# A running log-sum-exp over the rows of four matrices: loads and stores put into the DMA queue two at a time

## The chip, the cores and the metric

The kernel runs on one core of a Trainium2 chip. The metric is the device time of one execution in microseconds (us), lower is better. A core has five engines that run beside one another, each in its own program order: TensorE (PE, matrix multiply; its weight loads are listed as PEld), VectorE (DVE), ScalarE (ACT, functions of one argument), GpSimd (POOL) and SyncE (SP). In this kernel SP does nothing but issue DMAs. Sixteen DMA engines carry the data between the DRAM and the core's memory.

## The reference

The input `x` has the shape (4, 4096, 4128) in 32-bit floats: four batches of 4096 rows. Each output row is the logarithm of the sum of the exponentials of all rows up to it in its batch.

```python
def reference(x):
    B, S, D = x.shape
    out = np.zeros_like(x)
    out[:, 0, :] = x[:, 0, :].copy()
    for t in range(1, S):
        mx = np.maximum(out[:, t - 1, :], x[:, t, :])
        out[:, t, :] = mx + np.log(np.exp(out[:, t - 1, :] - mx) + np.exp(x[:, t, :] - mx))
    return out.astype(np.float32)
```

Every element is read once and written once, 270.53 MB each way.

## The kernel before

**Steps.** The rows of a batch are cut into steps. A step is 384 rows (128 partitions with r = 3 consecutive rows in each) or 256 rows (r = 2). A batch has ten steps of 384 rows and one of 256; the small one comes first in batch 0 and last in the others. There are 44 steps in all, numbered here from 0; the small ones are 0, 21, 32 and 43. A step of 384 rows moves 6192 KB in and as much out, a small one 4128 KB.

**Buffers.** A step lives in one tile `xt` of the pool `xpool`, which has `bufs = 4` buffers. `Step.load` (L132) fills it, the compute works in place, and `Step.store` (L135) writes it out. So load k+4 goes into the buffer of step k, and can't be issued before store k has landed. Both are issued on SP, one after another in the order in which the program emits them. A wait on SP holds up everything behind it on SP.

**Chunks.** The 4128 columns of a step are four chunks of 1024; the last chunk takes the remaining 32 columns (the tail) along. For each chunk:
- `exp` (L147, ACT) computes the exponentials in half precision over the front half of the same columns of the tile.
- `later` (L155, VectorE) adds the exponentials of the second and third row of each partition into the tile `sum`, when r is 3.
- `head` (L163 to L177, TensorE) builds in a PSUM tile `pt` the sum of all rows before the partition, the partition's first row, and the carry of the step before. `tail_head` does the same for the tail.
- `stage(j)` (L198) takes the logarithm of `pt` on ACT into row j of `xt`, then has TensorE add row j+1 (L201). After the last row it calls `keep` (L111, L112), which saves the running sum in `carry` for the next step, on VectorE. L203 is the logarithm of the tail.

**Order.** The schedule is written out by hand (`manual_schedule`): each engine runs its instructions in the order of emission, and the framework adds the waits on semaphores that the data needs. The main loop (L229) runs over all chunks g. In each iteration it emits `later` for chunk g+1, then `stage(2)` of chunk g-2, `stage(1)` of g-1 and `stage(0)` of g, then `exp` of chunk g+2 and `head` of g+1. So the last `stage` of a step stands on ACT behind the exps of the first chunks of the next step, and these need the next load.

**DMA order.** Four loads are issued ahead of the loop (L222, L223). When the last stage of step k has been emitted, the program emits store k and behind it load k+3, for k from 1 on (L236 to L240). SP's order is therefore: load 0, 1, 2, 3, store 0, store 1, load 4, store 2, load 5, and so on to store 40, load 43, store 41, store 42, store 43.

Of the kernel before, what the change touches and what calls it, by code (L numbers as in the profile page):

```python
# [50 lines left out]
def kernel(  # L51
# [23 lines left out]
    bufs = 4  # L75
# [132 lines left out]
    steps = []  # L208
# [9 lines left out]
        assert row == S  # L218

    chunks = [Chunk(s, c) for s in steps for c in range(n_main)]  # L220
    ahead = bufs - 1
    for s in steps[:bufs]:  # L222
        s.load()  # L223
    stored = 0
    chunks[0].exp()
    chunks[1].exp()
    chunks[0].later()
# [1 line left out]
    for g in range(len(chunks) + R - 1):  # L229
        if g + 1 < len(chunks):  # L230
            chunks[g + 1].later()
        for d in range(R - 1, -1, -1):
            if 0 <= g - d < len(chunks) and d < chunks[g - d].t.r:
                k = chunks[g - d]
                k.stage(d)
                if k.c == last and d + 1 == k.t.r:  # L236
                    k.t.store()
                    if bufs <= stored + ahead < len(steps):
                        steps[stored + ahead].load()
                    stored += 1  # L240
        if g + 2 < len(chunks):
            chunks[g + 2].exp()
        if g + 1 < len(chunks):
            chunks[g + 1].head()
# [30 lines left out]
```

## Time and profile before

| | |
|---|---|
| time, median of 3 runs | 1262.99 us (1262.85 to 1263.17) |
| the profiled execution: its own time | 1263.19 us |
| its span, first to last instruction | 1261.5 us |
| ACT busy | 947.3 us |
| PE busy | 661.2 us |
| DVE busy | 647.7 us |
| moved by DMA | 541.44 MB, mean 429 GB/s over the span |

The span is what the profile covers; the 1.7 us between it and the execution's own time lie around it. A group line of the profile gives: source line, engine, operation, output<-input, shapes, number of instructions, then busy time, mean duration in ns of one, and the idle time of the engine just before them with what ended most of it. A line of the timeline gives: start in us from the start of the span, length in us, engine, source line, operation, operands. For a DMA the length is that of its issue on SP (written SPq), not of the transfer; the DMA view gives the time from issue to landing, that is until the last of the 16 engines has reported:

| issued at L132 or L135 | number | KB each | median us from issue to landing |
|---|---|---|---|
| loads | 40 | 6192.0 | 42.3 |
| stores | 40 | 6192.0 | 28.1 |
| small loads | 4 | 4128.0 | 37.4 |
| small stores | 4 | 4128.0 | 29.7 |

A line of the waits gives: who waited, for whom, the total in us, how many times, and the longest.

### The profile page before, as it was taken

Reading aid. Unit: us, or ns where it says so; the run is one execution under the profiler, and the core shown is the slowest. Engines: PE = TensorE matmul, PEld = TensorE weight load, DVE = VectorE, ACT = ScalarE, POOL = GpSimd, SP = SyncE. Lnnn points to the kernel's source line nnn. Section 1 sums busy time; section 2 is a strip of 40 time slices with the busy share of each in tenths; the row PEclk is TensorE's granted clock in tenths of the full one; section 3 lists DMA queues with packets and bytes.
Section 4 is the critical chain, followed back from the end, with each engine's and each line's share of the span. In section 5 each row is a group of like instructions: output and inputs, shape, how many; then the busy total and the mean of one; then the engine's idle time right before and its main releaser. Section 6 shows DMA issues by size and latency. Waiting matters only on the chain. (4 is left out here: it accounts for less than half of the span.)

```text
span 1261.5 us, 5926 instructions
## 1 busy us (share of the span) xinstructions
PE 661.2 (52%) x1948; PEld 236.7 (19%) x1948; DVE 647.7 (51%) x606; ACT 947.3 (75%) x733; POOL 2.2 (0%) x13
## 2 busy tenths in 40 slices
PE   3655545465555555555446554555534655544562
PEld 1222111122121111211112121111111221111120
DVE  2674445554555545545446545544544645544454
ACT  5997777777777777778669777777866977777784
POOL 0000000000000000000000000000000000000000
PEclk9987676766577776768757677766775767787666
DMA  9999999999999999999999999999999999999998
GB/s 410 410 437 434 429 430 437 431 430 431 440 430 431 430 439 430 431 433 431 438 433 435 428 432 438 432 430 431 434 435 430 435 427 436 434 434 429 437 416 346
DMA packets 12702, 541.44 MB, mean 429 GB/s; under 512 B 1408, under 2 KB 1408, under 8 KB 1408
## 3 DMA queue, kind: packets, MB, share of 16 engines
q1 hardware_dynamic: 12672, 541.07, 99.4%
q8 instruction: 15, 0.25, 0.1%
q14 instruction: 15, 0.12, 0.0%
HBM read 270.53 MB, written 270.53 MB: 429 GB/s over the span
## 5 line engine op out<-in xcount | busy, mean ns | idle before, releaser
L147 ACT ACTIVATE xt<-xt 128x3072 f16<-128x3072 f32 (+3 forms) x176 | 478.3, 2717 | 248.4 <-DMA xt<-in_x_dram 248.4
L198 ACT ACTIVATE xt<-pt 128x1024 f32<-128x1024 f32 x512 | 487.5, 1029 | 2.5 <-PE pt L101 0.7
L155 DVE TENSOR_TENSOR sum<-xt 128x1024 fp32r<-128x1024 f16 x160 | 196.0, 1225 | 531.2 <-ACT xt L147 406.7
L97 PE MATMUL pt<-xt,ident 128*128 128x512 f16 x176 | 82.9, 471 | 482.8 <-ACT xt L198 482.8
L111 DVE CAST carry<-pt 32x1024 f16<-32x1024 f32 x176 | 216.4, 1230 | 46.4 <-ACT xt L198 41.3
L101 PE MATMUL pt<-xt,ident 128*128 128x512 f16 x496 | 209.5, 495 | 28.4 <-ACT xt L198 28.1
L112 DVE TENSOR_TENSOR carry<-pt,carry 32x1024 f16<-32x1024 f32 x176 | 215.9, 1226 | 6.1
L167 PE MATMUL pt<-sum,excl_r 128*128 128x512 f32 x320 | 198.7, 716 | 0.0
L101 PEld LDWEIGHTS <-ident 128*128 128x128 f16 x496 | 52.4, 106 | 646.5 <-issue 636.1
L97 PE MATMUL pt<-xt,incl 128*128 128x512 f16 x176 | 95.7, 544 | 71.7 <-DVE carry L112 54.0
L167 PEld LDWEIGHTS pt<-sum,excl_r 128*128 128x128 f32 x320 | 95.4, 298 | 48.4 <-issue 31.1
L101 PE MATMUL pt<-xt,incl 128*128 128x512 f16 x176 | 99.2, 564 | 0.0
L97 PE MATMUL pt<-carry,pick 128*128 128x512 f16 x160 | 84.4, 528 | 0.0
L101 PE MATMUL pt<-carry,pick 128*128 128x512 f16 x160 | 79.4, 496 | 0.0
L97 PEld LDWEIGHTS <-incl 128*128 128x128 f16 x220 | 23.7, 108 | 192.7 <-DVE carry L112 167.0
L203 ACT ACTIVATE xt<-qt 128x96 f32<-128x96 f32 (+1 forms) x44 | 10.9, 249 | 46.3 <-PE pt L101 46.3
L97 PEld LDWEIGHTS <-pick 128*128 128x128 f16 x200 | 24.2, 121 | 67.0 <-issue 66.3
L101 PEld LDWEIGHTS <-incl 128*128 128x128 f16 x260 | 27.6, 115 | 12.7 <-issue 9.2
L97 PEld LDWEIGHTS <-ident 128*128 128x128 f16 x176 | 21.4, 122 | 30.3 <-issue 24.3
L101 PEld LDWEIGHTS <-pick 128*128 128x128 f16 x160 | 20.5, 128 | 2.4 <-issue 1.7
L111 DVE CAST carry_t<-qt 32x32 f16<-32x32 f32 x44 | 8.7, 197 | 13.7 <-ACT xt L203 13.5
L97 PE MATMUL qt<-xt,incl 128*128 128x96 f16 (+1 forms) x44 | 10.6, 240 | 0.0
(25 smaller groups left out, 79.8 us busy)
## 6 DMA issues: line engine op xcount, KB each, us to landing
xt<-in_x_dram SPq DMA_DIRECT2D x40, 6192.0 KB, 42.3
out_dram<-xt SPq DMA_DIRECT2D x40, 6192.0 KB, 28.1
xt<-in_x_dram SPq DMA_DIRECT2D x4, 4128.0 KB, 37.4
out_dram<-xt SPq DMA_DIRECT2D x4, 4128.0 KB, 29.7
```

Source lines behind the costliest of these rows:

```text
L97: nc.tensor.matmul(pt, lhsT=w, rhs=rhs, start=start, stop=stop, skip_group_check=True)
L101: pe.add_instruction(mybir.InstMatmult(name=nc.get_next_instruction_name(), ins=[pe.lower_ap(rhs), pe.lower_ap(w, for_matmul_weights=True) ...
L111: nc.vector.tensor_copy(cr[HI:HI + 32, :], pt[HI:HI + 32])
L112: nc.vector.tensor_tensor(out=cr[LO:LO + 32, :], in0=pt[HI:HI + 32], in1=cr[HI:HI + 32, :], op=mybir.AluOpType.subtract,)
L147: nc.scalar.activation(self.t.half[:, :, 2 * c0:2 * c0 + w], self.t.xt[:, :, c0:c0 + w], ACT.Exp,)
L155: nc.vector.tensor_tensor(out=self.sum, in0=self.e(1, 0, CH), in1=self.e(2, 0, CH), op=mybir.AluOpType.add,)
L167: nc.tensor.matmul(pt[:, s:s + MM], lhsT=excl_r, rhs=self.sum[:, s:s + MM], start=False, stop=False, skip_group_check=True,)
L198: nc.scalar.activation(t.xt[:, j, c * CH:(c + 1) * CH], pt, ACT.Ln)
L203: nc.scalar.activation(t.xt[:, :, t0:D], self.qt, ACT.Ln)
```

## The change

Stores and loads are no longer emitted step by step. With `group = bufs // 2`, which is 2, nothing is emitted after an even step; after the last stage of an odd step k the program emits store k-1, store k, load k+3 and load k+4. SP's order becomes: load 0, 1, 2, 3, store 0, 1, load 4, 5, store 2, 3, load 6, 7, and so on to store 38, 39, load 42, 43, store 40, 41, store 42, 43. The buffers, the compute and its order on the other engines, `later` on VectorE among it, stay as they are.

```diff
@@ -218,10 +218,10 @@
     chunks = [Chunk(s, c) for s in steps for c in range(n_main)]
-    ahead = bufs - 1
+    group = bufs // 2
     for s in steps[:bufs]:
         s.load()
-    stored = 0
+    stored = done = 0
     chunks[0].exp()
@@ -234,10 +234,13 @@
                 k = chunks[g - d]
                 k.stage(d)
                 if k.c == last and d + 1 == k.t.r:
-                    k.t.store()
-                    if bufs <= stored + ahead < len(steps):
-                        steps[stored + ahead].load()
-                    stored += 1
+                    done += 1
+                    if done % group == 0 or done == len(steps):
+                        for s in steps[stored:done]:
+                            s.store()
+                        for s in steps[stored + bufs:done + bufs]:
+                            s.load()
+                        stored = done
```

## Prediction

> **What bounds the kernel now.** I read the page's summary first, then the chain of waits, then the DMA issues, and last the SP queue's waits and the timeline of its issues. Steps are numbered 0 to 43; steps 0, 21, 32 and 43 move 4128 KB each way, the others 6192 KB.
>
> ```profile
> span 1261.5 us, 5926 instructions
> PE 661.2 (52%) x1948; PEld 236.7 (19%) x1948; DVE 647.7 (51%) x606; ACT 947.3 (75%) x733; POOL 2.2 (0%) x13
> DMA  9999999999999999999999999999999999999998
> q1 hardware_dynamic: 12672, 541.07, 99.4%
> DMA 16%; ACT 5%; issue 1%; PE 1%; DVE 0%; SPq 0%; ACTq 0%
> L147 ACT ACTIVATE xt<-xt 128x3072 f16<-128x3072 f32 (+3 forms) x176 | 478.3, 2717 | 248.4 <-DMA xt<-in_x_dram 248.4
> ```
>
> The queue that SP feeds keeps the 16 DMA engines busy for 99.4% of the span. ACT, the busiest compute engine, is idle a quarter of it, and 248.4 us of that idleness is an exp waiting for a load. So the transfers bound the time, and an edit matters only if it lets the queue run dry, or changes how long a transfer takes.
>
> Is the queue really served back to back? The timeline of SP in mid-run (start, length, line):
>
> ```profile
> 292.29 0.37 SPq L132 DMA_DIRECT2D xt<-in_x_dram  x1
> 321.13 0.33 SPq L135 DMA_DIRECT2D out_dram<-xt  x1
> 321.57 0.37 SPq L132 DMA_DIRECT2D xt<-in_x_dram  x1
> 350.38 0.33 SPq L135 DMA_DIRECT2D out_dram<-xt  x1
> ```
>
> The DMA view, cut to each of these, gives 42.2, 28.0, 42.1 and 28.0 us to landing. So load 12 lands at 334.5, store 10 at 349.1, load 13 at 363.7, store 11 at 378.4: one transfer every 14.6 or 14.7 us, in the order of issue. When store 10 is issued, load 12 still has 334.5 - 321.1 = 13.3 us to run: that is the cover.
>
> What sets the issue of a store? Load 11 landed at 263.02 + 42.2 = 305.2, and store 10 went out 15.9 us later. ACT's timeline shows why: it stops 6.0 us before the first exp of step 11, and the last Ln of step 10 stands behind that exp on ACT. One step is then 276.02 to 299.3, some 23.3 us of ACT. So step k is done either 15.9 us after load k+1 lands (ACT waiting), or 23.3 us after step k-1 (ACT not waiting).
>
> **The change, part by part.** The instructions are the same: 44 loads, 44 stores, the same waits by buffer, the same compute. Only SP's order changes, from S10 L13 S11 L14 to S10 S11 L14 L15. A load still takes the buffer of the store four steps back, but now that store stands just ahead of it, not four issues ahead.
>
> *Waits on SP.* I place the new order on time, with T the landing of load 4. Loads 4 and 5 go in a pair, so load 5 lands at T+14.6. Behind load 5 SP comes to store 2. Load 2 landed a period of four transfers, 58.5 us, before T; steps 2 and 3 are 46.6 us of ACT, so ACT stands waiting when load 4 lands. By the two rules above, step 1 is done at T-58.5+15.9 = T-42.6, step 2 at T-42.6+23.3 = T-19.3, step 3 at T+15.9. Load 5 waits for store 1, which lands at T-14.6; store 2 follows it at once, and lands at T+29.2. Store 3 waits for step 3 until T+15.9 and is needed at T+29.2: cover 13.3 us, the same as now. Load 6 waits for store 2 to land at T+29.2; store 3 is then in flight, so the cover is 14.6 us. Load 7 waits for store 3, with load 6 in flight: 14.6 again. Store 4, behind load 7, is long done. Queued behind each waiting load on SP are only the next load and the next stores; who waits for them is ACT's next exp, which has 58.5 - 46.6 = 12 us per pair to spare. Cost 0.
>
> Without that cover a wait would cost the start of an empty queue: load 0, issued first, needs 12.3 us where a transfer of its size lands 9.7 us after the one ahead (the last store: 1245.28 + 15.3, against 1234.77 + 16.1), so 2.6 us each time.
>
> The trace has such a wait already:
>
> ```profile
> SPq L135 <- ACT xt L198: 1177.8, 44, 30.0
> SPq L132 <- DMA out_dram<-xt: 17.4, 5, 5.1
> ```
>
> Five loads do wait for a store to land. One is load 23, issued at 608.13, just as store 19 lands (584.53 + 23.5 = 608.0). Store 20 ahead of it lands at 606.45 + 31.0 = 637.5, load 23 at 608.13 + 43.9 = 652.0: 14.6 later. Nothing was lost. What the transfer ahead hides stays hidden.
>
> [...]
>
> *Issues.* 88 of 0.33 to 0.42 us in either order, under at least 13 us of queued work. Cost 0.
>
> *Runs of one direction.* The queue turns between reading and writing half as often. Loads alone: load 1 lands at 1.23 + 26.5 = 27.7, load 2 at 1.70 + 40.6 = 42.3, 14.6 apart. Store behind store: store 0 at 37.25 + 31.8 = 69.1, store 1 at 63.69 + 20.0 = 83.7, 14.6. Mixed, from store 2 (113.8) to store 40 (1183.01 + 28.4 = 1211.4) 38 pairs took 1097.6 us with four small transfers, each 4.9 shorter: (1097.6 + 19.6) / 38 = 29.4, against 2 x 14.6 = 29.2. If all of this 0.15 to 0.2 is turning, the gain has a bound of 0.15 x 39 = 6 us. On the other side, load 3, the last of the opening run, lands at 58.3, 16.0 after load 2: 1.4 us over. Should every read run end so, 20 x 1.4 = +28 us. The nearest rows are the many single handovers in mid-run at 14.6 to 14.7 either way, so I take -0.5.
>
> *Front and end.* The first two stores and load 4 are as now (load 4 waits for store 0 either way). At the end load 43 comes right behind load 42, so ACT's last wait goes:
>
> ```profile
> 1221.49 1.91 ACT L147 ACTIVATE xt<-xt 128x2048 f16<-128x2048 f32 x1 [1.64 <-DMA xt<-in_x_dram]
> ```
>
> Store 42 can then be issued up to 1.6 us before 1234.77. But store 41 lands at 1212.43 + 23.6 = 1236.0 and store 42 at 1250.9, 14.9 later where 14.6 is the floor: worth 0 to 0.3, I take 0.1.
>
> **Sum.** 0 + 0 - 0.5 - 0.1 = -0.6 us. The profiled execution took 1263.19 us (span 1261.5 and 1.7 around it), 0.2 over the median of 1262.99, so the forecast is 1262.99 - 0.6, rounded to 1262.5; its own range, from a third of the turning gain to a little new loss, is 1260.5 to 1265.
>
> **Rivals.** *The pair is one wait*: the first store of a pair leaves only when the second step is done. Then store 2 goes out at T+15.9, after load 5 has landed at T+14.6, into an empty queue: 15.9 + 2.6 - 14.6 = 3.9 us in each of 19 groups, 74 us; store 0 would go at 63.7 and land at 63.7 + 2.6 + 9.7 = 76.0, 7 late; store 42 would go at 1245.3 and the end come 1245.3 + 2.6 + 14.6 - 1250.9 = 11.6 late. In all +93, 1356 us. For it: the code emits both stores behind the last Ln of the second step. Against it: a store now waits for its own buffer, not for what was emitted before it. Step 10's last stage emits carry copies ahead of the store, and VectorE runs the first after it:
>
> ```profile
> 321.89 1.23 DVE L111 CAST carry<-pt 32x1024 f16<-32x1024 f32 x1
> ```
>
> The point of decision: it costs as soon as the first store leaves over 12.0 us (14.6 - 2.6) after the pair's first load lands.
>
> *A read run ends badly*, as load 3 did: +28, 1291 us. For it that one row; against it that load 3 ended at the first store of the kernel, and later handovers don't show it.
>
> *The engines drift apart*, and those ahead run dry while a load waits for the slowest engine's part of a store: from 1226 to 1236 the DMA share is 0.58, so by the end the mean engine stood 4.2 us idle waiting for store 42. The cover of 14.6 less 4.2 and 2.6 still leaves 8, and the slowest engine sets the end; a piece of it might cost 5 us, 1268.
>
> *Turning was the cost*: -6, 1257 us. For it the 0.2 us per pair; against it that the engines are 99.4% occupied as it is.
>
> **Chances.** Forecast 0.72, one wait for the pair 0.10, read runs 0.04, drift 0.05, turning 0.09. About 0.2%, 2.5 us, is what a measurement of this kernel can tell from no change. Under 1260.5 lie turning and a sliver of the forecast: 0.10. Over 1265.5 lie the first three rivals and a sliver: 0.20. Within: 0.70. The range from 1257.5 to 1268 takes in the forecast, half of turning and most of drift, and leaves some 0.18 outside.
>
> **What would show it.** SP's timeline: two stores, two loads; the first store of a pair right behind the second load, not 0.4 us ahead of its partner (else the first rival). Loads waiting for stores on SP for 13 to 15 us each, some 40 times, with landings still 14.6 apart (else turning, drift or read runs). The DMA share stays 1.00 and 433 GB/s in mid-run. ACT waits for loads once per pair, about twice as long each time, in the same total. The forecast is wrong if the DMA row drops below 9 in any slice before the last, or if the pair of transfers leaves 29.4 us.

## The result and the profile after

The changed kernel takes 1266.97 us (median of 7 runs, 1266.19 to 1268.04), against 1262.77 us for the kernel before (1262.68 to 1263.17): a ratio of 1.0032, with a 95% interval of 1.0021 to 1.0044. It is 4.2 us slower. The forecast was 1262.5 us, practically no change, so it was wrong: the time lies above the forecast's own range (1260.5 to 1265), though inside the wider one that it gave (1257.5 to 1268).

The page of the changed kernel, in the lines that answer to those shown of the kernel before. The profiled execution took 1268.04 us, the longest of the seven.

```profile
span 1266.3 us, 5926 instructions
PE 630.6 (50%) x1948; PEld 228.7 (18%) x1948; DVE 647.7 (51%) x606; ACT 945.3 (75%) x733; POOL 2.2 (0%) x13
DMA  9999999999999999999999999999999999999997
q1 hardware_dynamic: 12672, 541.07, 99.2%
DMA 70%; ACT 18%; issue 4%; PE 4%; DVE 2%; SPq 0%; ACTq 0%; DVEq 0%
L147 ACT ACTIVATE xt<-xt 128x3072 f16<-128x3072 f32 (+3 forms) x176 | 478.7, 2720 | 259.3 <-DMA xt<-in_x_dram 259.3
```

The compute has the same instructions, and the DMA row is as full as before up to the last slice. The page gives no hint of where 4.2 us went: the queue is busy nearly all the time, but the same bytes take longer. SP's timeline and its waits show the new order at work:

```profile
1053.88 15.22 SPq L132 DMA_DIRECT2D xt<-in_x_dram  x2
1069.20 30.36 SPq L135 DMA_DIRECT2D out_dram<-xt  x2
1112.93 15.19 SPq L132 DMA_DIRECT2D xt<-in_x_dram  x2
```

```profile
SPq L135 <- ACT xt L198: 660.2, 33, 29.9
SPq L132 <- DMA out_dram<-xt: 511.9, 38, 19.6
```

Two loads, two stores. The second load of a pair goes out at 1068.77, and the first store right behind it at 1069.20. Loads wait for a store to land 38 times, 13.5 us on average, and until the last stores the slowest engine always had work.

To find the time one must leave the page for the landings. A transfer lands when the last of its 16 DMA engines reports (the page counts 1408 packets under 512 bytes, 16 for each of the 88 transfers). The even-numbered loads have exactly the same transfers ahead of them in both kernels, so their landings can be compared. The table gives, from the records of the trace, when the 15th and the 16th engine reported (us):

```
              before             after         16th engine,
           15th      16th     15th      16th   after - before
load 8    216.36   216.96   215.11   215.88      -1.08
load 20   568.57   568.61   567.36   570.03      +1.42
load 30   852.71   853.13   851.48   855.24      +2.11
load 34   964.84   966.05   965.25   969.40      +3.35
load 38  1076.94  1078.87  1078.53  1083.30      +4.43
load 42  1194.56  1196.56  1196.34  1201.34      +4.78
store 43 1260.54  1260.62  1263.44  1265.47      +4.85
```

The changed kernel is 1.08 us ahead at load 8 and loses 5.9 us from there to the end. Until load 30 the 15th engine is no later than before; one engine falls behind alone, by 3.8 us at load 30. Between loads 30 and 38 all engines lose time. At the end the lag is passed on: store 42 waits for step 42, step 42 for load 42, so store 42 is issued at 1237.67 instead of 1234.77, and the other engines wait for work with it.

The packets of that one engine can be followed, each starting 3 ns before the one ahead ends. A packet of 49,536 bytes normally takes 1829 ns, eight make a transfer. Its load packets mostly do (the table of all traces below has 26 ns over per load before and 15 after). These are the ns over 1829 of the store packets, with the instructions that PE, PEld, DVE and ACT ran in that time (in two windows each; an instruction that crosses the bound between them counts in both, and counted once they are 52, 89 and 70):

```
                          packets 1 to 8               sum   instructions
before, store 39 (1166.7) 15  5  0 44 33 33 15 43      188   57
after,  store 36 (1097.4) 27 33 15 43 43 43 52 43      299   91
after,  store 37 (1112.4) 32 38  5 33 43 33 33 33      250   72
```

The instruction counts come from these windows (bounds, length, then busy time and count of PE, PEld, DVE, ACT, POOL; granted clock; DMA share; GB/s), first the kernel before, the first three packets of store 39 and the other five:

```profile
1166.70:1172.20 5.50, 0.40 (x2) 0.12 (x2) 2.21 (x2) 5.04 (x4) 0.00 (x0) 0.56 1.00 432
1172.20:1181.50 9.30, 7.21 (x17) 2.36 (x16) 5.55 (x7) 8.20 (x7) 0.00 (x0) 0.50 0.99 426
```

and the changed kernel, stores 36 and 37:

```profile
1097.40:1103.00 5.60, 3.32 (x12) 1.40 (x12) 3.68 (x3) 5.60 (x5) 0.00 (x0) 0.94 1.08 469
1103.00:1112.40 9.40, 4.69 (x23) 1.76 (x22) 6.69 (x6) 9.01 (x8) 0.00 (x0) 0.97 1.02 443
1112.40:1117.90 5.50, 3.18 (x8) 1.08 (x7) 2.86 (x5) 4.76 (x5) 0.00 (x0) 0.75 0.97 417
1117.90:1127.20 9.30, 6.83 (x18) 2.47 (x17) 5.57 (x5) 9.27 (x7) 0.00 (x0) 0.72 1.00 431
```

Before, 10 instructions run under the first three packets, and these are hardly lengthened; 47 run under the other five. In store 36 it is 32 and 59. The reason is where the compute pauses. In the kernel before it pauses once per step, as a load ends and a store begins: ACT has just begun again, and PE is still idle:

```profile
1171.81 0.59 PE L97 MATMUL pt<-xt,ident 128*128 128x512 f16 x1 [7.51 <-ACT xt L198]
```

In the changed kernel it pauses once per pair, twice as long, and the pause lies under loads (this load lands at 1083.3, the stores come 14.6 us later):

```profile
1083.38 2.76 ACT L147 ACTIVATE xt<-xt 128x3072 f16<-128x3072 f32 x1 [13.86 <-DMA xt<-in_x_dram]
```

So theory A, formed here: **each instruction that the compute engines run lengthens the store packets of one DMA engine by some 3 ns** (188 / 57, 299 / 91, 250 / 72 give 3.3, 3.3 and 3.5; with each instruction counted once, 3.4 to 3.6), the load packets of that engine hardly at all. The pairs put the busy time of the compute under the stores and its pause under the loads.

### The profile page after: what moved, and what is told of

Same layout as the page of the kernel before. It is cut to its first block, busy times and chain, and to the rows that moved or that the text cites. A ratio compares the mean times of both kernels' runs of the same rounds, so it can differ in the third digit from the quotient of the medians.

```text
span 1266.3 us, 5926 instructions
## 1 busy us (share of the span) xinstructions
PE 630.6 (50%) x1948; PEld 228.7 (18%) x1948; DVE 647.7 (51%) x606; ACT 945.3 (75%) x733; POOL 2.2 (0%) x13
## 2 busy tenths in 40 slices
DMA packets 12702, 541.44 MB, mean 428 GB/s; under 512 B 1408, under 2 KB 1408, under 8 KB 1408
## 3 DMA queue, kind: packets, MB, share of 16 engines
q1 hardware_dynamic: 12672, 541.07, 99.2%
## 4 chain that ended last, share of the span: by engine, by line
DMA 70%; ACT 18%; issue 4%; PE 4%; DVE 2%; SPq 0%; ACTq 0%; DVEq 0%
DMA out_dram<-xt 40%; DMA xt<-in_x_dram 30%; ACT xt L198 9%; ACT xt L147 8%; PE pt L101 2%; PE pt L97 1%; DVE carry L111 1%; DVE carry L112 1%; DVE sum L155 0%; PE pt L167 0%; ACT xt L203 0%; SPq L132 0%; ACTq L273 0%; ACTq L147 0%; ACTq L203 0%
## 5 line engine op out<-in xcount | busy, mean ns | idle before, releaser
L97 PE MATMUL pt<-xt,ident 128*128 128x512 f16 x176 | 77.5, 440 | 501.2 <-ACT xt L198 501.1
L101 PE MATMUL pt<-xt,ident 128*128 128x512 f16 x496 | 200.2, 470 | 36.2 <-ACT xt L198 35.9
L167 PE MATMUL pt<-sum,excl_r 128*128 128x512 f32 x320 | 191.8, 693 | 0.0
L97 PE MATMUL pt<-xt,incl 128*128 128x512 f16 x176 | 92.1, 523 | 79.0 <-DVE carry L112 61.6
L167 PEld LDWEIGHTS pt<-sum,excl_r 128*128 128x128 f32 x320 | 91.9, 287 | 45.4 <-issue 27.3
L101 PE MATMUL pt<-xt,incl 128*128 128x512 f16 x176 | 95.6, 543 | 0.0
L97 PE MATMUL pt<-carry,pick 128*128 128x512 f16 x160 | 82.5, 516 | 0.0
L101 PE MATMUL pt<-carry,pick 128*128 128x512 f16 x160 | 76.8, 480 | 0.0
L97 PEld LDWEIGHTS <-ident 128*128 128x128 f16 x176 | 20.9, 119 | 28.8 <-issue 22.4
```

The lines of the kernel that those rows point to most:

```text
L97: nc.tensor.matmul(pt, lhsT=w, rhs=rhs, start=start, stop=stop, skip_group_check=True)
L101: pe.add_instruction(mybir.InstMatmult(name=nc.get_next_instruction_name(), ins=[pe.lower_ap(rhs), pe.lower_ap(w, for_matmul_weights=True) ...
L167: nc.tensor.matmul(pt[:, s:s + MM], lhsT=excl_r, rhs=self.sum[:, s:s + MM], start=False, stop=False, skip_group_check=True,)
```

## The experiments

**No compute.** Everything but the loads and stores is left out, in the order of before (shown) and in that of after.

```diff
-    chunks = [Chunk(s, c) for s in steps for c in range(n_main)]
...
-    for g in range(len(chunks) + R - 1):
...
+    for s in steps:
+        s.store()
+        if bufs <= stored + ahead < len(steps):
...
```

> Leaves out all compute: loads and stores alone, in the order of before (store k, load k+3), the same 88 transfers. Theory A (one DMA engine's store packets take some 33 ns longer while the compute engines run many instructions; pairs put all eight packets of a store under them, singles about five): no store packet is lengthened, stores land 14.6 us apart like loads, time about 1254 us. Theory B (a run of two transfers in one direction is slower in itself): stores and loads as in before, time near 1262.

> The same without compute, in the order of after (two stores, two loads). Theory A: the same time as the singles without compute, within 1 us, about 1254. Theory B: 4 us over the singles, stores landing 14.9 us apart. Theory C (DMA engines ahead run dry while a load waits for the slowest one's part of a store): some us over the singles, with idle engines between the transfers.

Measured: 1258.39 us in singles (ratio to before 0.9965, 0.9952 to 0.9978) and 1257.84 in pairs (0.9960, 0.9945 to 0.9974). Without compute the pairs cost nothing; half a microsecond, if anything, is gained. The order of the transfers by itself is not the cause, and theory B is out. The time that theory A gave, about 1254, was missed by 4 us. Both are 4.4 to 4.9 us faster than the kernel before, whose queue also never runs dry before 1228 us: a full queue is not yet a queue at its fastest.

**Less compute on PE and DVE.** Of the products on TensorE only the first of each chunk and its tail is kept, of VectorE's work only the adds of `later`; ACT keeps all its instructions.

```diff
-            if t.r == 3:
...
-                    mm(pt[:, s:s + MM], pick, carry[self.c][:, s:s + MM])
...
-                    mm(pt[:, s:s + MM], ident, self.e(j + 1, s, s + MM), stop=j + 2 == t.r)
...
-                keep(carry[c], pt)
```

> The order of before; leaves out the carry between steps and partitions' later rows: TensorE does only the first product of each chunk, VectorE no carry copies; exp and Ln on ACT are as before. About a third of the instructions stay, ACT stays as busy. Theory A: 1256 to 1259 us. Theory B: 1262 to 1263. If ACT's reading and writing is what lengthens the packets (A'), 1262 to 1263 as well.

> The order of after with the same work left out. Theory A: 1257 to 1260 us, at most 1.5 us over the lean singles, store landings nearer 14.7 than 14.9 us. Theory B: 4 us over the lean singles, about 1267. A': 1266 to 1267.

Measured: 1260.15 us in singles and 1260.13 in pairs (both 0.9981, 0.9971 to 0.9990). The difference between the orders is gone here too (theory A gave up to 1259 and 1260, B and A' 1262 and more). The second kernel's page, and its loads' waits for stores on SP:

```profile
span 1258.3 us, 2417 instructions
PE 184.8 (15%) x480; PEld 57.8 (5%) x480; DVE 198.1 (16%) x166; ACT 939.3 (75%) x733; POOL 2.2 (0%) x13
```

```profile
SPq L132 <- DMA out_dram<-xt: 559.4, 40, 20.6
```

ACT is nearly as busy as ever and still writes all of the tile, with 2417 instructions in all instead of 5926. So it is not what ACT moves, nor that loads wait for stores on SP, that costs the 4 us. One thing besides the instructions differs from the changed kernel: in mid-run no engine runs dry here, while there some do at 985 us (see the second effect below). Summed over all engines and three windows of mid-run, the lengthening of the packets that are 12 to under 90 ns over, per load and store of a step:

```
               instructions per us   ns per load and store
copy_singles          0.00                  40
copy_pairs            0.00                  47
lean_singles          1.44                 119
lean_pairs            1.47                 138
before                4.21                 183
after                 4.14                 259
```

The last two rows have the same number of instructions and differ by 76 ns: it is not only how many, but what they run beside.

**Sparing one engine.** Store 20 is issued in two parts, partitions 0 to 119 and the rest, so that one engine would be given less to do, in both orders. (The first kernel has 1415 packets under 512 bytes where the kernel before has 1408: 7 more, which is what reports of 15 and 8 engines instead of 16 would make.)

```diff
+            if self is steps[20]:
+                nc.sync.dma_start(out=d[:120], in_=self.xt[:120])
+                nc.sync.dma_start(out=d[120:], in_=self.xt[120:])
```

> The order of before, whole computation; store 20 goes as two DMAs, partitions 0 to 119 and 120 to 127, which by their shapes may be spread over 15 and 8 DMA engines and so spare one engine 8 packets, 14.6 us. If the one that lags is the one spared, the last landings come 2 us earlier (the next engine lags 2.0 us less when load 42 lands): about 1260.8 us. If it is another one, no gain, up to 1.8 us more (eight engines carry one packet more): 1262.7 to 1264.6.

> The order of after, whole computation, with the same split of store 20. If the engine that lags is the one spared: its 5.0 us behind the next one at load 42 go, and the time comes to 1262.5 to 1264, about that of before. This is what theory A asks for, since under it the loss of 4.2 us sits in one engine alone. If another engine is spared: 1267 to 1269. If the loss sits in all engines: 1267.

Measured: 1278.50 us (1.0121, 1.0106 to 1.0136) and 1278.42 (1.0126, 1.0109 to 1.0143), 15.7 us worse than the kernel before. In the first kernel the two parts of the split store landed 24.7 and 28.8 us after the load ahead of them, where a whole store takes 14.7; that is more than the split could save. The lagging engine of the second kernel was still 1.4 to 2.7 us behind the next one from load 24 on. Inconclusive: which engine lags, and whether it is the one that was spared, stays open.

**Instructions by kind.** The copy in pairs, with stretches in which one engine alone runs many short or few long instructions on data of its own, with no tie to the transfers: DVE 1600 times 32 columns (the diff shows it) and 160 times 1024, PE 1600 times 64 and 420 times 512, ACT 900 times 32 and 190 times 1024.

```diff
+    for i in range(1600):
+        nc.vector.tensor_tensor(out=d32[:, :32], in0=a16[:, :32], in1=a16[:, 32:64],
+                                op=mybir.AluOpType.add)
...
```

> Loads and stores alone in the order of after, all compute left out, while the engines run padding on constants, one phase after another: VectorE 1600 adds of 32 columns, then 160 of 1024; TensorE 1600 products of 64 columns, then 420 of 512; ACT 900 exps of 32 columns, then 190 of 1024. Theory A (number of instructions): store packets of one DMA engine are lengthened in each phase in proportion to instructions per us, much in the phases of short instructions, a few ns in those of long ones, loads not at all, whichever engine runs them. Theory A'' (the bytes that engines read and write): the long phases at least as much as the short ones. Theory A-PE: TensorE's phases alone.

Measured, in one execution: 1270.37 us. The windows of its stretches, in the order DVE short, DVE long, PE short, PE long, ACT short, ACT long:

```profile
100.00:360.00 260.00, 0.00 (x0) 0.00 (x0) 220.82 (x1152) 0.00 (x0) 0.00 (x0) 1.00 1.00 432
375.00:560.00 185.00, 0.00 (x0) 0.00 (x0) 179.94 (x148) 0.00 (x0) 0.00 (x0) 1.00 1.00 428
570.00:650.00 80.00, 54.27 (x1568) 51.54 (x1566) 0.00 (x0) 0.00 (x0) 0.00 (x0) 0.94 1.00 428
660.00:735.00 75.00, 75.00 (x349) 34.05 (x348) 0.00 (x0) 0.00 (x0) 0.00 (x0) 1.00 0.99 417
740.00:960.00 220.00, 0.00 (x0) 0.00 (x0) 0.00 (x0) 193.19 (x844) 0.00 (x0) 0.50 1.00 429
985.00:1180.00 195.00, 0.00 (x0) 0.00 (x0) 0.00 (x0) 189.37 (x180) 0.00 (x0) 0.50 1.00 434
```

The store packets of the one engine took, beside 4.4 short DVE instructions per us, 1.865 us (36 ns over); beside 3.84 short ACT instructions, 1.861 (32 over); beside 4.65 long matmuls and as many weight loads, 1.876 (47 over); beside 19.6 short matmuls and as many weight loads, 2.042 (213 over). Beside 0.80 long DVE or 0.92 long ACT instructions per us, which keep their engine as busy (179.94 of 185 us and 189.37 of 195) and work on far more columns per us (0.80 x 1024 against 4.4 x 32 on DVE), the store packets were only some 10 ns over. Beside the short instructions and the matmuls that is 2.7 to 4.5 ns per instruction. In these stretches the number of instructions counts, on each of the three engines, not how busy the engine is. This shows the effect with no wait and no data shared between compute and queue.

**More instructions in the real kernel.** The kernel before, with either 38 short copies (0.17 us each) or 6 long reductions (1.22 us each) put on DVE into the pause of each step, on data of their own.

```diff
+        if g + 2 < len(chunks) and chunks[g + 2].c == 0:
+            for _ in range(38):
+                nc.vector.tensor_copy(pad[:, 64:96], incl[:, :32])
```

```diff
+            for _ in range(6):
+                nc.vector.tensor_reduce(
+                    out=pad[:, 96:104], in_=incl.unsqueeze(1).to_broadcast([P, 8, P]),
...
```

> The order of before, whole computation, and in each step 38 copies of 32 columns on VectorE (0.19 us each, 7.2 us) put into the pause in which the compute engines wait for the next load, in which the first three of a store's eight packets per DMA engine leave. Theory A (number of instructions while a store leaves): the first three packets of each store on the one engine are lengthened by some 30 ns too, 3 x 30 ns x 42 = 3.8 us: 1265.5 to 1267.5, nearly all that pairing cost, without any pairing. If instructions don't matter, or only those of TensorE: 1262.5 to 1263.5. If the padding only hurts by holding up the compute, fill_long is as late.

> The same with six reductions of 1024 elements per partition (some 1.2 us each, 7.2 us) in place of the 38 short copies: VectorE as busy in the pause, a sixth of the instructions. Theory A: 6 instructions more in 7 us, 1262.7 to 1263.6. If being busy or reading the core's memory is what counts: as fill_small, 1265.5 or more.

Measured: 1282.05 us (1.0153, 1.0139 to 1.0167) and 1271.04 (1.0070, 1.0056 to 1.0084). Both miss what was expected: the filling also held up the first steps (store 1 landed 3.8 and 2.8 us late), those around the small steps, and the last store. The pair was run again with the filling in 28 steps of mid-run alone (5 to 19, 24 to 30, 35 to 40), the rest unchanged:

> fill_small with the 38 short copies in 28 steps of mid-run alone (5 to 19, 24 to 30, 35 to 40), so that the padding holds up neither the first steps, nor those around a small step, nor the end. Theory A: the slowest engine's pairs of a load and a store take 0.1 to 0.3 us longer there (the spread because the padding's own instruction fetches fall on one engine too): 28 x 0.1 to 0.3 = 3 to 8 us, 1265.5 to 1270.5. If instructions don't matter: 1262.5 to 1263.2.

> fill_long with the six reductions in the same 28 steps alone. Theory A: 1262.6 to 1263.6, the time of before. If VectorE being busy or reading the core's memory is what counts: as fill_small_mid.

Measured: 1268.87 us (1.0048, 1.0034 to 1.0062) with the copies, 1263.26 (1.0004, 0.9995 to 1.0013) with the reductions. The same stretch of DVE's timeline, first with copies, then with reductions:

```profile
359.88 7.90 DVE L250 COPY pad<-incl 128x32 f16<-128x32 f16 x38
```

```profile
358.90 7.49 DVE L250 TENSOR_REDUCE pad<-incl 128x8 f16<-128x1024 f16 x6
```

DVE is held for nearly as long by both, 7.9 and 7.5 us, and only the many instructions cost much time: 6.1 us against 0.5. From load 26 to load 30 a load and a store of the slowest engine took 29.75 us with copies and 29.39 with reductions, against 29.35 in the kernel before and 29.51 in the changed one. That DVE is held is not the cost; that it runs more instructions is. But not all of the 6.1 us is the lengthening of theory A: half of the copies ran under loads, and the tables below give stores only 49 ns more each, some 2 us in all, while packets that are 90 ns and more over cost a mean engine 3.5 us more than before. The kernel with copies has 23 packets in the queue q14, which the page calls instruction, where the one before has 15; whether they have a part in this was not tested.

**A later start.** The last experiment tries to turn the theory into a gain: hold the compute back by a long DVE instruction on the fresh load, so that the pause moves further under the store, in 32 steps.

```diff
+            if k.c == 0 and (g + 2) // n_main in late:
+                nc.vector.tensor_reduce(
+                    out=pad, in_=k.t.xt[:, 0, :CH].unsqueeze(1).to_broadcast([P, 4, CH]),
+                    op=mybir.AluOpType.max, axis=mybir.AxisListType.X,
+                )
             k.exp()
```

> The kernel before, unchanged in what it computes and in its DMA order, with one VectorE reduction of 4 x 1024 elements (an estimate of 4.9 us, four times the 1.22 us of a 1024-element one) over the first chunk of a freshly landed load, in 32 steps; the exp of that chunk must wait for it. So ACT, TensorE and VectorE start each step 4.9 us later, and the pause of the compute, which in the kernel before covers the first three of eight packets of the store on the lagging engine (10 instructions in 5.5 us, then 47 in 9.3 us), covers about five of them. The cover of a store falls from 13.3 to 8.4 us. Theory A (the lagging engine's store packets lengthen with the instructions that the compute engines run meanwhile, its load packets do not): some 18 fewer instructions run under each such store; from the lengthening of the three stores shown (about 185 ns at 57 instructions, 299 at 91, 250 at 72, that is 3.2 to 3.5 ns each) 58 ns less per store, 32 x 58 = 1.9 us: 1260.9 us, ratio 0.9985, with lengthened packets of about 130 ns per pair of transfers against 183. Theory B (it is the number of instructions per pair of transfers that counts, wherever they fall): no change, 1262.8 us, ratio 1.000, 183 ns. Theory C (a later start uses up the cover, engines run dry): slower than 1263.5 us.

Measured: 1267.16 us (1.0036, 1.0022 to 1.0049), slower: the outcome of theory C, against A's estimate. The reduction took 4.42 us and ACT started that much later. But the windows of one store (5.5 us, then the rest, some 0.6 us behind its packets) show that the premise failed:

```profile
1171.10:1176.60 5.50, 1.72 (x12) 0.95 (x13) 4.59 (x2) 0.84 (x1) 0.00 (x0) 0.90 1.00 432
1176.60:1185.80 9.20, 4.69 (x10) 1.49 (x10) 4.58 (x6) 8.10 (x7) 0.00 (x0) 0.51 1.01 436
```

28 and 33, that is 61 instructions under a store instead of the 40 hoped for: PE's work of the step before was pushed under the store as well. The packets of this store were 20, 43, 5, 9, 5, 33, 33 and 43 ns over, 191 in sum or 3.1 per instruction, so the size per instruction fits A, but nothing is told apart between A and B: in the three windows the packets are 205 ns over per load and store, neither A's 130 nor B's 183. Most of the 4.3 us came from elsewhere: loads 22 and 33 took 16.10 and 15.67 us between landings where 14.6 is usual, behind two stretches (589 to 591 and 904 to 907 us) in which the faster engines had run dry around the small steps. That is the second effect, and the changed kernel has it too.

**All traces together.** What the late start was to show can be read from the runs themselves. For transfers 8 to 83 (in the order of issue, between 100 and 1220 us) the table counts the instructions of PE, PEld, DVE and ACT that ended while the slowest engine carried out a store or a load, and sums the ns of all packets 12 to under 90 over that ended in that time:

```
                 per store:               per load:            ns per instruction,
                 instructions   ns over   instructions  ns over    stores
copy_singles          0.0          5          0.0         41         -
copy_pairs            0.0         11          0.0         28         -
lean_singles         21.2         85         21.3         27        4.0
lean_pairs           30.5        118         11.7         15        3.9
before               50.1        161         70.1         26        3.2
fill_long_mid        51.8        168         72.7         52        3.2
late_start           56.8        155         64.7        105        2.7
fill_small_mid       64.7        210         83.4         52        3.2
after                76.9        257         42.7         15        3.3
```

This is the pairs' doing over the whole run, not only in the three stores above: 27 instructions moved from each load to each store, and a store is 96 ns longer for it, a load not shorter by nearly as much. The late start, too, put more instructions under the stores, not fewer.

**The second effect** was found in the traces, not by an experiment of its own: bursts of a microsecond or so in which 9 to 22 packets, on most engines at once, are 0.2 to 1.6 us over. In mid-run the trace of the changed kernel has three, the kernel before none of such a size. (Near 54 us, in load 3, every trace has one of 0.8 to 1.2 us; it is the long end of load 3 that the prediction saw.) Mean loss per engine, with the stretches in which engines had run dry ahead of them:

```
                  dry ahead     bursts at (us): mean loss per engine (us)
after             -             914.3: 1.25
after             985 to 987    999.0: 0.46    1027.2: 0.92
late_start        589 to 591    603.2: 0.42    618.4: 1.10
late_start        904 to 907    919.0: 0.54    934.2: 0.91
fill_small_mid    902 to 904    916.3: 0.48    931.5: 1.01
fill_long         67 to 70      82.6: 0.66     97.9: 1.15
fill_small        67 to 71      83.6: 0.72     98.9: 0.89
fill_small        909 to 911    923.8: 0.51    939.0: 0.89
fill_small        995 to 997    1008.9: 0.49   1022.8: 0.79
```

Where engines run dry in mid-run and start again together, one burst follows some 14 to 17 us later and another 14 to 28 us after that. It isn't the whole rule: the burst at 914.3 follows no such stretch, though load 33 went out at 899.73, only 1.2 us before the first engine was done with load 32; other bursts, some in the kernels with filling and in the one with stretches, have nothing of the kind ahead; and a dry stretch near the end (1217 to 1219 in the changed kernel, 1228 to 1236 before) has none behind it. No run took this effect away by itself, and its cause stays open.

The two effects side by side, from 100 to 1220 us (us; in the copies the 2.0 are spread over all engines):

```
                 packets 12 to under 90 ns over,   packets 90 ns and more over,   median time
                 sum of all engines                mean of an engine              against before
copy_pairs                2.0                            1.0                         -4.9
lean_pairs                5.5                            1.0                         -2.6
before                    7.6                            1.6                          -
fill_long_mid             8.9                            2.1                         +0.5
fill_small_mid           10.7                            5.1                         +6.1
late_start               10.1                            6.1                         +4.3
after                    11.1                            4.1                         +4.2
```

## Why the prediction was wrong, step by step

*Waits on SP: right for the order, wrong for the cover at the small steps.* The pair is not one wait; the first rival is false (store 4 went out at 142.68, right behind load 7 at 142.24). Loads wait as worked out, and land 14.6 us behind the transfer ahead. But the cover was worked out for full steps alone. Store 33 stands behind small store 32, and stores 40 and 41 behind small load 43: stores 33 and 41 went out at 985.32 and 1217.26, as the faster engines ran dry; up to eight and six of the 16 stood idle for about a microsecond. The lagging engine did not run dry, so this cost nothing directly; the bursts behind 985 us may be its price.

*Issues: right*, though one issue took 0.54 us, not at most 0.42. *Front and end: right in the mechanism*: store 42 is issued 36.3 us after load 42 lands instead of 38.2, 1.9 us sooner where up to 1.6 was foreseen (and 0.1 taken), but load 42 itself lands 4.8 us later.

*Runs of one direction: the step that failed.* It took 29.4 us per load and store against twice 14.6, had only "turning" as a reason for the 0.15 to 0.2 us between them, and took -0.5 for it. It had no term for what the compute runs while a store is carried out. The copies show that nearly all of it is not turning: with no compute, singles take 29.25 per pair (load 38 to load 42) and pairs 29.25 too. In the kernel before, the same stretch takes 29.42, in the changed one 29.51. The 0.17 is the lengthening of one engine's stores by the compute's instructions (161 ns per store), and it grew where the step expected it to shrink (257 ns). That the copies differ by 0.55 us, about the -0.5 taken, is luck: no row gave that size. The prediction's own sign fired, since the pair left 29.4 us (29.51 from load 26 to load 30).

*The size.* In the profiled execution the 38 stores behind load 8 make 38 x 0.096 = 3.6 us, and the bursts 1.19 (load 33) + 0.96 (load 37) = 2.15 on the lagging engine. The sum, 5.8, stands against the 5.9 lost from load 8 (1.08 ahead) to the last store (4.85 behind); why the changed kernel is ahead at load 8 is not shown. Of the 5.9, 3.2 were lost by load 30, ahead of the first burst. So the larger part has its cause in the experiments, and the bursts, over a third, have none. The profiled execution is the slowest of the seven. If the bursts differ from one execution to the next, that would explain why the changed kernel's runs spread over 1.85 us and those of before over 0.49; this is argued, not shown, as only one of the seven has a trace.

*The drift rival* came nearest: it named the slowest engine and 1268 us. But its mechanism, engines ahead that run dry and wait, was not the one that cost most; the slowest engine grew slower by itself. It should have been read in the trace of before: the 15th and 16th engine 2.0 us apart at load 42, and stores that took 14.82 us between landings late in the run against 14.60 for loads. The prediction rounded both to "14.6 or 14.7".

*Turning was the cost* is false: the copies differ by 0.5 us. *A read run ends badly* is false as a rule: in the copy in pairs no load but load 3 ends so. But what befell load 3 came back twice in the changed kernel, in loads 33 and 37, both the second of a pair and some 1.0 and 0.9 us late between landings. The single loads 22 and 33 of the late start were met by the same kind of burst, so the end of a read run isn't its condition.

## What to carry to other kernels

When a queue is full and bounds the kernel, look at the landings engine by engine: the mean busy share, 99.2% here, hid the one engine that set the end (2.0 us behind the 15th at store 43). Time was lost there by how many instructions ran beside the stores (77 instead of 50, 257 ns over per store instead of 161), so a reordering that left the bytes and the instructions alone, and whose waits stayed covered in the steady run, cost 0.3%, the larger part of it by moving the compute's pause from stores to loads. Check also the cover of a new order at the odd-sized steps, not only in the steady run.

## What the runs showed of the hardware

In these runs one of 16 DMA engines carried out its stores more slowly while the compute engines ran instructions: 36 ns over 1829 beside 4.4 DVE instructions per us, 213 beside 39 matmuls and weight loads per us, some 10 beside 0.8 long DVE instructions per us. Its loads were hardly touched (26 ns over per load in the kernel before, 15 in the changed one), nor were the other 15 engines: at load 30 the 15th of the changed kernel was no later than that of the kernel before (851.48 us against 852.71). Why one engine, and whether it would be there in an execution of which no trace is taken, no run here shows.

The amount of data that the compute engines moved did not show in these runs: six long reductions per step left a store at 168 ns over against 161. The number of instructions did: 257 against 161, with 77 instructions beside a store against 50. Where the packets are held up, no run here shows.

The packets that the page calls instruction meet the queue as well: with each of the 15 of the queue q8 (16,384 bytes each) one data packet took 0.37 to 0.55 us longer, in the kernel before and in the changed one. And a store of 120 of 128 partitions with one of the other 8 behind it landed 24.7 and 28.8 us after the transfer ahead, where the whole took 14.7.
